# The seam between the two MLP multiplications: four preparations of operands placed behind the last evictions, slice 7's sums behind them, and VectorE's instructions there in the order of the source

## The chip, the cores and the metric

The kernel runs on one core of one Trainium2 chip. The metric is the device time of one execution in microseconds. Engines are named as in the profile: PE is TensorE's matrix multiplication, PEld its weight load, DVE is VectorE, ACT is ScalarE, POOL is GpSimd, SP is SyncE, which here issues the DMA transfers.

## The reference

One layer of a streaming encoder: a normalised input goes through two kinds of attention, an output projection and an MLP with a squared ReLU, each with a residual sum. The sequence has 1024 positions, the model 1024 channels, the MLP 4096 hidden ones, all in float32. The change lies in the MLP alone:

```python
def reference(x, ..., norm2_g, w_ff1, w_ff2, final_norm_g):
    ...
    h = h + jnp.einsum('bsm,md->bsd', y, w_out[layer])
    n2 = rms_norm(h, norm2_g[layer])
    u = jnp.square(jax.nn.relu(jnp.einsum('bsd,df->bsf', n2, w_ff1[layer])))
    h = h + jnp.einsum('bsf,fd->bsd', u, w_ff2[layer])
    return rms_norm(h, final_norm_g)
```

## The kernel before

**Numbers.** Each float32 operand of the MLP is split into two fp16 parts. A high half is a rounded copy that ACT makes; a low half is what remains, made by DVE or POOL. One multiplication then takes three fp16 matmuls (`mm3`). `split` (L1404) issues both: ACT first scales or copies (L1408, L1410), then POOL subtracts (L1412), or DVE subtracts and scales in one instruction (L1414).

**Strassen.** Both MLP multiplications work on 2 x 2 blocks with seven products in place of eight, numbered 1 to 7, in the order 1, 5, 6, 3, 7, 2, 4. The operands of a product are blocks or differences of blocks. `second_operands` (L1387) makes the differences (L1384, DVE), which are called T for the first multiplication's weights and Z for the second's.

**First multiplication.** The hidden channels are cut into eight slices n = 0 to 7. `product1(n, p)` (L1435) runs the 24 matmuls of product p of slice n, from X and W, into a PSUM tile f, and then evicts it. The PSUM tile of product 1 is used again by 6, 7 and 4, that of product 5 by 3; product 2 has its own. Products 1, 5 and 6 are copied by ACT into kept tiles k. Products 3, 7 and 2 are evicted by DVE, which adds a kept tile and takes the largest value (L1473, into topf), and then squares (L1475). Product 4 goes through ACT into v, twice, and DVE finds its largest value (L1471). Behind product 4 stand the slice's **sums**, four additions or subtractions of kept tiles on DVE (L1484 to L1490), and short instructions for the scale (L1495, L1496, L1189). Each finished block of u, the squared activations, is stored to DRAM (ud). The stores stand in SP's queue in the written order, since `queue[0]` is there an `InOrder` object (L151): a wrapper that ties each instruction it issues behind the one before. ACT has the same wrapper during the first multiplication (`act1[0]`, from the ninth product on). DVE hasn't: what is given to it straight is ordered by the scheduler.

**Second multiplication.** `order2` (L1582) lists group g, product p and slice n; four groups of two slices each. One product of one slice takes 24 matmuls from V and U into a chain f_a, f_b or f_c; two slices make the 48 that a row of the trace shows together. DVE adds each finished chain into an accumulator C (`add_up`, L1733). `prepare2(at)` (L1637) makes the **pieces** for entry `at` of `order2`: U from a block u that was loaded from ud, and V from a block of the second weights or a difference Z of two. Both are split as above. U's low half is POOL's work, but DVE's for product 5. `fetch2` loads blocks u, through SP, a few entries ahead.

**The seam.** While slice 7 of the first multiplication runs, the first pieces of the second are made. `FIRST_PIECES` (L47) says behind which product of slice 7 each of the first four is made: entries 0 to 3 are product 1 of slices 0 and 1 and product 5 of slices 0 and 1. `FIRST_LOADS` says the same of the loads and isn't touched. The main loop (L1652 to L1682) calls `prepare1`, which makes the weights W of a product some places ahead, then `product1`, then the rest. After it stand `load_acc` (L1687), which loads the accumulators C, and the groups of the second multiplication.

In names such as k7_6, W7_2, U0_5 or Z1_6 the first number is the slice and the second the product; C001 is half 1 of block (0, 0).

Of the kernel before, what the change touches and what calls it, by code (L numbers as in the profile page):

```python
# [24 lines left out]
NQ = DFF // (4 * P)  # L25
# [20 lines left out]
}  # L46
FIRST_PIECES = {(7, 1): 0, (7, 5): 1, (7, 6): 2, (7, 3): 3}  # L47
START_FILL = 3
A_FILL = 7
B_FILL = [13, 13, 9.5, 9.5] * 2 + [11.25] * 8  # L50
# [15 lines left out]
def kernel(  # L66
# [29 lines left out]
    nc = tc.nc  # L96
# [411 lines left out]
    dve, pool = nc.vector, nc.gpsimd  # L508
# [576 lines left out]
    for j in range(4):  # L1085
        Q, K, V = [], [], []
        fill.add(f"B{j}", in_proj(KB0 + j * P, "k", f"kB{j}", K, None))
        q, v = (QB0 + j * P, "q", f"qB{j}", Q, None), (VB0 + j * P, "v", f"vB{j}", V, None)
# [50 lines left out]
    def flat(t):  # L1139
        return t.rearrange("p a b -> p (a b)")  # L1140

    def page2(shape, name, dt=F32):
        return mp.tile(shape, dt, tag="pg2", bufs=10, name=name)

    def tst(shape, name):
        return main.tile(shape, F32, tag="tst", bufs=TST, name=name)
# [3 lines left out]
    def page16(shape, name, alloc=None):  # L1150
        return (alloc or page)(shape, name, F16)
# [63 lines left out]
    def pair_psum(name):  # L1215
        return mps.tile([P, 2, HALF], F32, tag="ab", bufs=3, name=name)
# [154 lines left out]
    def scaled1(n, *blocks):  # L1371
        up1, left = to_scale1[n]
        for b in blocks:
            if b in left:
                left.remove(b)
                w = w1s[(n, *b)]
                act1[0].activation(w, w, AF.Copy, scale=up1)
# [9 lines left out]
    def second_operands(src, made, p, name, engine, alloc):  # L1387

        if p == 1:
            return src(0, 0)  # L1390
        if p == 2:
            return src(1, 0)
        if p == 3:
            return src(1, 1)
        a, b = {
            5: lambda: (src(0, 1), src(0, 0)),
            6: lambda: (src(1, 1), made[5]),
            7: lambda: (src(1, 1), src(0, 1)),
            4: lambda: (src(1, 0), made[6]),
        }[p]()  # L1400
        made[p] = sum_of(a, b, ALU.subtract, name, engine, alloc)
        return made[p]

    def split(full, name, engine, alloc, up=None):  # L1404
        w = alloc(name)
        w = [w[:, hl] for hl in range(2)]
        if up is not None and engine is pool:
            act1[0].activation(full, full, AF.Copy, scale=up)  # L1408
            up = None
        act1[0].activation(w[0], full, AF.Copy, scale=1.0 if up is None else up)  # L1410
        if up is None:
            engine.tensor_tensor(w[1], full, w[0], ALU.subtract)  # L1412
        else:
            engine.scalar_tensor_tensor(w[1], full, up, w[0], ALU.mult, ALU.subtract)  # L1414
        return w
# [3 lines left out]
    def prepare1(n, p, at):  # L1419
        if n >= NQ or (n, p) in wops:  # L1420
            return
        made = wsum.setdefault(n, {})
        if n:
            scaled1(n, *{1: ((0, 0), (0, 1)), 5: ((0, 1), (1, 1)), 6: ((1, 1), (1, 0))}.get(p, ((1, 0), (0, 1), (1, 1))))
        second = page2 if at < 2 or at > 4 else page1
        t = second_operands(
            lambda i, j: w1s[n, i, j], made, p, f"T{n}_{p}", dve, lambda name: second([P, 4, 2 * P], name)
        )
        wops[n, p] = split(
            t, f"W{n}_{p}", dve if at < 7 and at != 2 else pool, lambda name: page16([P, 2, 4, 2 * P], name), None if n else to_scale1[0][0]  # L1430
        )
# [3 lines left out]
    def product1(n, p):  # L1435
        a, c = chains.setdefault(n, [None, None])
        if p in (1, 5, 2):
            ps = pair_psum(f"f1_{n}_{p}")
            if p == 1:
                chains[n][0] = ps  # L1440
            if p == 5:
                chains[n][1] = ps
        else:
            ps = c if p == 3 else a
        hi, lo = wops.pop((n, p))
        for u in range(2):
            cols = slice(u * P, (u + 1) * P)
            for k in range(4):
                x2 = [X[p][k // 2][:, hl, k % 2] for hl in range(2)]
                mm3(ps[:, u], (hi[:, k, cols], lo[:, k, cols]), x2, k == 0 and p in (1, 5, 2), k == 3, True)  # L1450
                if k % 2:
                    turn()
        while stores:
            stores.pop(0)()
        kept = saved.setdefault(n, {})
        ps = flat(ps)
        if p in (1, 5, 6):
            if p == 5 and n:
                kept[p] = tst([P, 2 * HALF], f"k{n}_{p}")
            else:  # L1460
                kept[p] = page2([P, 2 * HALF], f"k{n}_{p}")
            act1[0].activation(kept[p], ps, AF.Copy)
            return
        v = tst([P, 2 * HALF], f"v{n}") if p == 4 else kept[{3: 6, 7: 5, 2: 1}[p]]
        if n not in topf:
            topf[n] = small.tile([P, 4], F32, tag="topf", bufs=2, name=f"topf_{n}")
        top = topf[n][:, {3: 0, 7: 1, 2: 2, 4: 3}[p] :][:, :1]
        if p == 4:
            act1[0].activation(v, ps, AF.Relu)
            act1[0].activation(v, v, AF.Square)  # L1470
            dve.tensor_reduce(top, ps, mybir.AxisListType.X, ALU.max)  # L1471
        else:
            dve.tensor_tensor_reduce(v, ps, v, 1.0, 0.0, ALU.add, ALU.max, top)  # L1473
            if n:
                dve.scalar_tensor_tensor(v, v, 0.0, v, ALU.max, ALU.mult)  # L1475
            else:
                act1[0].activation(v, v, AF.Relu)
                act1[0].activation(v, v, AF.Square)
        if p != 4:
            put(n, {3: 2, 7: 4, 2: 1}[p], v)  # L1480
            return

        u00, u01, u11, u10 = kept[1], kept[6], kept[5], v
        dve.tensor_tensor(u11, u10, u11, ALU.add)  # L1484
        put(n, 5, u11)
        dve.tensor_tensor(u10, u00, u10, ALU.subtract)
        put(n, 7, u10)
        dve.tensor_tensor(u00, u11, u00, ALU.subtract)
        put(n, 6, u00)
        dve.tensor_tensor(u01, u01, u00, ALU.subtract)  # L1490
        put(n, 3, u01)
        if n % GQ == 0:
            topu[n // GQ] = Top(f"u{n // GQ}", NQ + n // GQ, GQ)
        top, col = topf.pop(n), topu[n // GQ].column()
        nc.vector.tensor_reduce(col, top, mybir.AxisListType.X, ALU.max)  # L1495
        nc.vector.tensor_tensor(col, col, down1[n], ALU.mult)  # L1496
        if n % GQ == GQ - 1:
            topu[n // GQ].gather()
# [138 lines left out]
    def prepare2(at):  # L1637
        if at >= len(order2) or order2[at][1:] in ready2:
            return
        g, p, n = order2[at]  # L1640
        ready2.add((p, n))
        alloc = page if at <= 3 * GQ else page3
        high = lambda name: page16([P, 2, 2, HALF], name, alloc)
        temp = lambda name: alloc([P, 2, HALF], name, F32)
        a = u2s.pop((n, p))
        b = second_operands(lambda i, j: w2s[n, i, j], made_b.setdefault(n, {}), p, f"Z{n}_{p}", dve, temp)
        ops2[n, p] = (
            split(a, f"U{n}_{p}", dve if p == 5 else pool, high, uup[n]), split(b, f"V{n}_{p}", dve, high, up2[g])
        )

    queue[0] = InOrder(nc.sync)
    for at, (n, p) in enumerate(order1):  # L1652
        if at == 8:
            act1[0] = InOrder(nc.scalar)
        if p == (1 if n > 1 else 5) and n:
            load1(n + 1)
        ahead1 = at + (AHEAD1 + 1 if at < AT_ONCE else AHEAD1)

        behind = (n, p) == (0, 2)
        if ahead1 < len(order1) and not behind:  # L1660
            prepare1(*order1[ahead1], ahead1)
        product1(n, p)
        for work in chores.get((n, p), ()):
            combined(*work)
            if behind and work[0] == 5:
                prepare1(*order1[ahead1], ahead1)
        if 0 < n < NQ - 1:
            if p == 3:
                see1(n + 1)
            if p == 7:  # L1670
                scale1(n + 1)
        if p == 3 and n and n % GQ == 0:
            scale_of_u(n // GQ - 1)
        if at > 6:
            look2(at, p != 1)
        for i, blocks in FIRST_LOADS.get((n, p), ()):
            if i is not None:
                fetch2(i)
            for tile2 in blocks:
                load2w(*tile2)  # L1680
        if (n, p) in FIRST_PIECES:
            prepare2(FIRST_PIECES[n, p])  # L1682
    assert not to_see and not on_way and not to_scale
    act1[0] = nc.scalar
    acc = {}

    def load_acc(i, j):  # L1687
# [147 lines left out]
    g, p, n0 = order2[-GQ]  # L1835
# [104 lines left out]
```

## Time and profile before

| What | Value |
|---|---|
| Time, median of 3 runs | 1032.37 us (1030.7 to 1033.74) |
| The profiled execution's own time | 1034.48 us |
| Its span, first to last instruction | 1032.7 us |
| Mean granted TensorE clock | 0.994 |
| DMA, mean over the span | 194 GB/s |

The profile shows one execution. In a row of the timeline stand the start, the length in us, the engine, the line, the operation, the tiles it writes and reads ("out<-in", numbers left out), and the count of instructions that were drawn together. Brackets at the end give the idle time of the engine before the row and what ended it: "[1.74 <-POOL W L1412]" means that the engine stood still for 1.74 us until POOL had written W in line 1412. Rows of one engine overlap a little, since its instructions are pipelined: the next begins shortly before the length given has passed. The columns of the windows are told where they are shown.

### The profile page before, as it was taken

What the parts mean: (1) busy time and instruction counts of PE and PEld (TensorE: products, weight loads), DVE (VectorE), ACT (ScalarE), POOL (GpSimd) and SP (SyncE); (2) the same over time, 40 slices, a digit from 0 to 9 for tenths busy, and PEclk for the clock granted to TensorE, in tenths of its full rate; (3) what the DMA queues carried; (4) which work ended last, traced back from release to release, by engine and by line L of the source; (5) the groups of instructions that cost most, each with busy time, mean ns of one, the idle gap of its engine ahead of it and who ended that gap; (6) DMA issues with size and microseconds to landing.
All of it is one profiled execution on the core that took longest, in us unless ns stands there. A gap on an engine that the chain in (4) does not pass through costs nothing. (4 is left out here: it accounts for less than half of the span.)

```text
span 1032.7 us, 14046 instructions
## 1 busy us (share of the span) xinstructions
PE 997.6 (97%) x4818; PEld 590.7 (57%) x4818; DVE 805.6 (78%) x1288; ACT 650.5 (63%) x1060; POOL 448.9 (43%) x341
## 2 busy tenths in 40 slices
PE   9999999999979999989999999999899999999997
PEld 7888887777756668644444444444344444444443
DVE  5576787867675738995989999979886887686976
ACT  8676766766576745676646655756286655557446
POOL 0466665242452472106335444446163243345333
PEclk9999999999989999999999999999999999999999
DMA  9944527999999894205778668738699454443004
GB/s 355 267 126 130 139 77 186 192 211 228 211 248 225 201 304 159 86 21 183 252 257 285 218 228 288 248 141 304 223 299 401 142 181 137 169 162 123 1 1 163
DMA packets 150567, 200.63 MB, mean 194 GB/s; under 512 B 78688, under 2 KB 96224, under 8 KB 150496
## 3 DMA queue, kind: packets, MB, share of 16 engines
q1 hardware_dynamic: 150352, 199.47, 64.0%
q8 instruction: 38, 0.62, 0.3%
q14 instruction: 33, 0.27, 0.1%
q10 hardware_dynamic: 144, 0.26, 0.1%
HBM read 120.01 MB, written 42.99 MB: 158 GB/s over the span
## 5 line engine op out<-in xcount | busy, mean ns | idle before, releaser
L179 PE MATMUL f<-X,W 128*128 128x512 f16 x1344 | 294.5, 381 | 6.2 <-DVE topf L1473 3.9
L179 PEld LDWEIGHTS <-W 128*128 128x128 f16 x1344 | 131.6, 98 | 164.0 <-issue 7.5
L179 PEld LDWEIGHTS <-U 128*128 128x128 f16 x1356 | 132.4, 98 | 160.6 <-ACT V L1410 1.8
L1412 POOL TENSOR_TENSOR U<-u,U 128x1024 f16<-128x1024 f32 x48 | 120.9, 2531 | 167.7 <-ACT U L1410 157.3
L179 PE MATMUL f_a<-V,U 128*128 128x512 f16 x756 | 165.3, 379 | 0.9 <-DVE C L1733 0.9
L1412 POOL TENSOR_TENSOR W<-T,W 128x1024 f16<-128x1024 f32 x29 | 73.4, 2532 | 82.6 <-ACT W L159 49.4
L1412 POOL TENSOR_TENSOR W<-w,W 128x1024 f16<-128x1024 f32 x21 | 49.4, 2353 | 90.1 <-ACT W L159 69.2
L1408 ACT ACTIVATE u<-u,uupn 128x1024 f32<-128x1024 f32 x46 | 52.1, 1144 | 56.2 <-DMA u<-ud 55.3
L179 PE MATMUL f_c<-V,U 128*128 128x512 f16 x384 | 84.2, 379 | 1.4 <-DVE C L1733 1.4
L1414 DVE SCALAR_TENSOR_TENSOR V<-Z,up,V 128x1024 f16<-128x1024 f32 x32 | 52.3, 1638 | 28.2 <-ACT V L1410 23.3
L631 ACT ACTIVATE P_B<-P_B,nm_B 128x640 f32<-128x640 f32 (+2 forms) x64 | 44.2, 691 | 32.0 <-DVE nm_B L628 16.5
L1410 ACT ACTIVATE U<-u 128x1024 f16<-128x1024 f32 x46 | 48.1, 1045 | 25.6 <-DVE Z L1384 11.3
L179 PE MATMUL op_A<-w_o,y 128*128 128x512 f32 x192 | 58.6, 430 | 5.7 <-DVE ts_vB L441 5.1
L876 DVE SCALAR_TENSOR_TENSOR H_B<-P_B,rc_B,H_B 128x640 f16<-128x640 f32 (+2 forms) x64 | 50.8, 822 | 13.7 <-ACT H_B L871 13.3
L179 PE MATMUL ip_qB<-nT,w_qB 128*128 128x512 f32 x192 | 53.8, 406 | 1.1 <-DVE t_kB L415 1.0
L1414 DVE SCALAR_TENSOR_TENSOR V<-w,up,V 128x1024 f16<-128x1024 f32 x24 | 42.9, 1791 | 14.8 <-ACT V L1410 7.8
L179 PE MATMUL ip_kB<-nT,w_kB 128*128 128x512 f32 x192 | 53.7, 405 | 0.0
L179 PE MATMUL ip_vB<-nT,w_vB 128*128 128x512 f32 x192 | 51.3, 400 | 0.0
L159 ACT ACTIVATE w<-w,up 128x1024 f32<-128x1024 f32 x24 | 26.7, 1137 | 38.5 <-DVE up L1162 38.5
L179 PE MATMUL ip_qA<-nT,w_qA 128*128 128x512 f32 x192 | 50.5, 397 | 0.3 <-DVE VA L185 0.3
L1410 ACT ACTIVATE V<-Z,up 128x1024 f16<-128x1024 f32 x30 | 34.1, 1137 | 25.4 <-DVE Z L1384 24.8
L871 ACT ACTIVATE H_B<-P_B,rc_B 128x640 f16<-128x640 f32 (+2 forms) x64 | 40.8, 685 | 9.9 <-DVE rc_B L868 4.5
(295 smaller groups left out, 2007.1 us busy)
## 6 DMA issues: line engine op xcount, KB each, us to landing
w<-in_w_ff_dram SPq DMA_DIRECT2D x64, 512.0 KB, 7.2
u<-ud SPq DMA_DIRECT2D x56, 512.0 KB, 5.7
ud<-k SPq DMA_DIRECT2D x48, 512.0 KB, 3.6
m<-in_w_ff_dram SPq DMA_DIRECT2D x32, 512.0 KB, 5.9
KkB<-t_kB SPq DMA_DIRECT2D x32, 256.0 KB, 5.1
xr<-in_x_dram SPq DMA_DIRECT2D x8, 512.0 KB, 9.2
st_o<-in_w_out_dram SPq DMA_DIRECT2D x8, 512.0 KB, 4.3
h<-in_x_dram SPq DMA_DIRECT2D x8, 512.0 KB, 4.9
```

What stands on the lines that cost most here:

```text
L159: ins = getattr(self.engine, op)(*args, **kw)
L179: pe(nc.tensor.matmul(*args, **kw))
L631: nc.scalar.activation(pr, pr, AF.Exp, bias=nm, scale=-1.0, accum_out=sm)
L871: nc.scalar.activation(hi, q, AF.Copy, scale=rc)
L876: nc.vector.scalar_tensor_tensor(lo, q, rc, hi, ALU.mult, ALU.subtract)
L1408: act1[0].activation(full, full, AF.Copy, scale=up)
L1410: act1[0].activation(w[0], full, AF.Copy, scale=1.0 if up is None else up)
L1412: engine.tensor_tensor(w[1], full, w[0], ALU.subtract)
L1414: engine.scalar_tensor_tensor(w[1], full, up, w[0], ALU.mult, ALU.subtract)
```

## The change

Three things are moved, and nothing is added or taken away. Entries 2 and 3 of the pieces (product 5 of slices 0 and 1) are made behind products 2 and 4 of slice 7, no longer behind 6 and 3. The sums of a slice stand in a function `finish1`, called at once for slices 0 to 6; slice 7's are called behind its last pieces. From ahead of slice 7's product 7 to the end of the loop, `dve` is an `InOrder` object, so what it issues in that stretch keeps the written order.

```diff
-FIRST_PIECES = {(7, 1): 0, (7, 5): 1, (7, 6): 2, (7, 3): 3}
+FIRST_PIECES = {(7, 1): 0, (7, 5): 1, (7, 2): 2, (7, 4): 3}
...
             put(n, {3: 2, 7: 4, 2: 1}[p], v)
             return
 
+        last_sums.append(lambda: finish1(n, kept, v))
+        if n < NQ - 1:
+            last_sums.pop()()
+
+    last_sums = []
+
+    def finish1(n, kept, v):
+
         u00, u01, u11, u10 = kept[1], kept[6], kept[5], v
         dve.tensor_tensor(u11, u10, u11, ALU.add)
...
             prepare1(*order1[ahead1], ahead1)
+        if (n, p) == (NQ - 1, 7):
+            dve = InOrder(nc.vector)
         product1(n, p)
...
         if (n, p) in FIRST_PIECES:
             prepare2(FIRST_PIECES[n, p])
+        if (n, p) == (NQ - 1, 4):
+            last_sums.pop()()
     assert not to_see and not on_way and not to_scale
     act1[0] = nc.scalar
+    dve = nc.vector
```

**VectorE, from product 3's eviction of slice 7 on.** ISA rows are the evictions (the short one reads the largest value), "k<-k" the squares, U and V the low halves of pieces. In the kernel before:

```order
L1414 SCALAR_TENSOR_TENSOR U0_5_7055<-u0_5_6944,uupn_0_5570,U0_5_7055 128x1024
L1473 ISA k7_6_7045,topf_7_7088<-f1_7_5_6962,k7_6_7045 128x1024
L1473 ISA topf_7_7088 128x1
L1414 SCALAR_TENSOR_TENSOR V0_5_7058<-Z0_5_7053,up2_0_5795,V0_5_7058 128x1024
L1475 SCALAR_TENSOR_TENSOR k7_6_7045<-k7_6_7045 128x1024
L1414 SCALAR_TENSOR_TENSOR U1_5_7093<-u1_5_6948,uupn_1_5572,U1_5_7093 128x1024
L1414 SCALAR_TENSOR_TENSOR V1_5_7096<-Z1_5_7091,up2_0_5795,V1_5_7096 128x1024
L1473 ISA k7_5_6987,topf_7_7088<-f1_7_1_6913,k7_5_6987 128x1024
L1473 ISA topf_7_7088 128x1
L1475 SCALAR_TENSOR_TENSOR k7_5_6987<-k7_5_6987 128x1024
L1473 ISA k7_1_6942,topf_7_7088<-f1_7_2_7131,k7_1_6942 128x1024
L1473 ISA topf_7_7088 128x1
```

In the changed kernel, where instructions that the wrapper issues carry line 159 (U0_6 and so on follow further down):

```order
L1473 ISA k7_6_7045,topf_7_7080<-f1_7_5_6962,k7_6_7045 128x1024
L1473 ISA topf_7_7080 128x1
L1475 SCALAR_TENSOR_TENSOR k7_6_7045<-k7_6_7045 128x1024
L159 ISA k7_5_6987,topf_7_7080<-f1_7_1_6913,k7_5_6987 128x1024
L159 ISA topf_7_7080 128x1
L159 SCALAR_TENSOR_TENSOR k7_5_6987<-k7_5_6987 128x1024
L159 ISA k7_1_6942,topf_7_7080<-f1_7_2_7115,k7_1_6942 128x1024
L159 ISA topf_7_7080 128x1
L159 SCALAR_TENSOR_TENSOR k7_1_6942<-k7_1_6942 128x1024
L159 TENSOR_TENSOR Z0_5_7143<-w2_0_01_6946,w2_0_00_6901 128x1024
L159 SCALAR_TENSOR_TENSOR U0_5_7145<-u0_5_6944,uupn_0_5570,U0_5_7145 128x1024
L159 SCALAR_TENSOR_TENSOR V0_5_7148<-Z0_5_7143,up2_0_5795,V0_5_7148 128x1024
```

The evictions of products 3, 7 and 2 (k7_6, k7_5, k7_1) stand together now, with no piece of product 5 between them, and the pieces follow. Then come topf's reduction, Z1_5, U1_5 and V1_5, and after them the four sums. Behind the sums the two instructions on C000 and C001 now stand ahead of Z0_6 and Z1_6; before, Z0_6 stood first.

**ScalarE, at the same place.** U and V are high halves of pieces, W those of the first multiplication's weights, k7_6 the copy of product 6, and u a block that is scaled in place. Before:

```order
L159 ACTIVATE W7_7_7018<-T7_7_7016 128x1024
L159 ACTIVATE k7_6_7045<-f1_7_1_6913 128x1024
L159 ACTIVATE U0_5_7055<-u0_5_6944,uupn_0_5570 128x1024
L159 ACTIVATE V0_5_7058<-Z0_5_7053,up2_0_5795 128x1024
L159 ACTIVATE W7_2_7061<-w1_7_10_6618 128x1024
L159 ACTIVATE U1_5_7093<-u1_5_6948,uupn_1_5572 128x1024
L159 ACTIVATE V1_5_7096<-Z1_5_7091,up2_0_5795 128x1024
L159 ACTIVATE W7_4_7101<-T7_4_7099 128x1024
L1408 ACTIVATE u0_6_7007<-u0_6_7007,uupn_0_5570 128x1024
L1408 ACTIVATE u1_6_7051<-u1_6_7051,uupn_1_5572 128x1024
L159 ACTIVATE v7_7184<-f1_7_1_6913 128x1024
```

In the changed kernel:

```order
L159 ACTIVATE W7_7_7018<-T7_7_7016 128x1024
L159 ACTIVATE k7_6_7045<-f1_7_1_6913 128x1024
L159 ACTIVATE W7_2_7053<-w1_7_10_6618 128x1024
L159 ACTIVATE W7_4_7085<-T7_4_7083 128x1024
L1408 ACTIVATE u0_6_7007<-u0_6_7007,uupn_0_5570 128x1024
L1408 ACTIVATE u1_6_7051<-u1_6_7051,uupn_1_5572 128x1024
L159 ACTIVATE U0_5_7145<-u0_5_6944,uupn_0_5570 128x1024
L159 ACTIVATE V0_5_7148<-Z0_5_7143,up2_0_5795 128x1024
L159 ACTIVATE v7_7176<-f1_7_1_6913 128x1024
L159 ACTIVATE v7_7176<-v7_7176 128x1024
L159 ACTIVATE U1_5_7182<-u1_5_6948,uupn_1_5572 128x1024
L159 ACTIVATE V1_5_7185<-Z1_5_7180,up2_0_5795 128x1024
```

W7_2 and W7_4 come right behind the copy of product 6, and the pieces of product 5 come behind the scaling of u0_6 and u1_6; U1_5 and V1_5 stand behind both instructions on v.

**ScalarE, in the second multiplication's second group.** The changed code doesn't name this place; the scheduler puts the rows there. Before:

```order
L1410 ACTIVATE U3_5_7782<-u3_5_7633,uupn_3_6168 128x1024
L1410 ACTIVATE V3_5_7785<-Z3_5_7780,up2_1_6182 128x1024
L1408 ACTIVATE u2_4_7960<-u2_4_7960,uupn_2_6166 128x1024
L1410 ACTIVATE U2_6_7818<-u2_6_7672 128x1024
L1410 ACTIVATE V2_6_7822<-Z2_6_7816,up2_1_6182 128x1024
L1410 ACTIVATE U3_6_7855<-u3_6_7705 128x1024
L1408 ACTIVATE u3_4_7997<-u3_4_7997,uupn_3_6168 128x1024
L1410 ACTIVATE V3_6_7859<-Z3_6_7853,up2_1_6182 128x1024
L1410 ACTIVATE U2_3_7892<-u2_3_7740 128x1024
L1408 ACTIVATE u4_1_8036<-u4_1_8036,uupn_4_6771 128x1024
```

In the changed kernel:

```order
L1408 ACTIVATE u3_2_7923<-u3_2_7923,uupn_3_6168 128x1024
L1410 ACTIVATE V3_5_7785<-Z3_5_7780,up2_1_6182 128x1024
L1410 ACTIVATE U2_6_7818<-u2_6_7672 128x1024
L1408 ACTIVATE u2_4_7960<-u2_4_7960,uupn_2_6166 128x1024
L1410 ACTIVATE V2_6_7822<-Z2_6_7816,up2_1_6182 128x1024
L1408 ACTIVATE u3_4_7997<-u3_4_7997,uupn_3_6168 128x1024
L1410 ACTIVATE U3_6_7855<-u3_6_7705 128x1024
L1408 ACTIVATE u4_1_8036<-u4_1_8036,uupn_4_6771 128x1024
L1410 ACTIVATE V3_6_7859<-Z3_6_7853,up2_1_6182 128x1024
L1410 ACTIVATE U2_3_7892<-u2_3_7740 128x1024
```

U2_6 has moved from behind u2_4 to ahead of it, and u4_1 from behind V3_6 to ahead. From V2_3 on, which comes next, ACT's order is that of before, and in the third and fourth groups DVE's is too. The orders of POOL and SP are unchanged throughout.

## The prediction

> **What bounds the kernel now.** I began with the page's busy shares:
>
> ```profile
> PE 997.6 (97%) x4818; PEld 590.7 (57%) x4818; DVE 805.6 (78%) x1288; ACT 650.5 (63%) x1060; POOL 448.9 (43%) x341
> ```
>
> PE is busy for 97% of the span, so a change elsewhere counts only where PE waits or runs slowly. The second view is PE's timeline around the seam of the two MLP multiplications, and then its rows to the end.
>
> ```profile
> 700.11 16.14 PE L179 MATMUL f<-X,W 128*128 128x512 f16 x74
> 717.99 4.92 PE L179 MATMUL f<-X,W 128*128 128x512 f16 x22 [1.74 <-POOL W L1412]
> 726.81 6.91 PE L179 MATMUL f<-X,W 128*128 128x512 f16 x24 [3.90 <-DVE topf L1473]
> 733.56 10.52 PE L179 MATMUL f_a<-V,U 128*128 128x512 f16 x48
> ```
>
> ```profile
> 754.28 10.52 PE L179 MATMUL f_a<-V,U 128*128 128x512 f16 x48
> ...
> 920.04 10.52 PE L179 MATMUL f_a<-V,U 128*128 128x512 f16 x48
> ...
> 961.48 10.52 PE L179 MATMUL f_b<-V,U 128*128 128x512 f16 x48
> 973.38 10.52 PE L179 MATMUL f_c<-V,U 128*128 128x512 f16 x48 [1.38 <-DVE C L1733]
> ```
>
> The 74 matmuls end with slice 7's product 7. Product 2 (717.99) waited 1.74 us for POOL's low half of W, product 4 (726.81) 3.90 us for DVE's eviction of product 7, whose PSUM tile it writes into. Then the second multiplication runs without a wait up to 972. Product 4 was slow as well. From 733.56 to 754.28, 20.72 us, 96 matmuls run, so 24 take 5.18; its 24 took 6.75 (726.81 to 733.56). The windows say why; the columns after the length and five busy times are granted clock, DMA share and GB/s:
>
> ```profile
> 726.80:729.00 2.20, 2.19 (x6) 0.80 (x6) 2.20 (x2) 0.00 (x0) 0.00 (x0) 0.50 0.07 28
> 729.00:731.00 2.00, 2.00 (x9) 0.76 (x8) 1.38 (x3) 0.00 (x0) 0.00 (x0) 0.74 0.57 231
> ```
>
> The clock was 0.50 and then 0.74: 2.20 x 0.50 + 2.00 x 0.26 = 1.6 us lost. The seam costs PE 1.74 + 3.90 + 1.57 (6.75 less 5.18) = **7.21 us**.
>
> Why they came late stands in the rows of ACT, POOL and DVE:
>
> ```profile
> 705.49 1.02 ACT L159 ACTIVATE k<-f 128x1024 f32<-128x1024 f32 x1
> 710.84 1.15 ACT L159 ACTIVATE U<-u,uupn 128x1024 f16<-128x1024 f32 x1 [4.32 <-DMA u<-ud]
> 713.33 1.15 ACT L159 ACTIVATE V<-Z,up 128x1024 f16<-128x1024 f32 x1 [1.34 <-DVE Z L1384]
> 714.38 1.04 ACT L159 ACTIVATE W<-w 128x1024 f16<-128x1024 f32 x1
> ```
>
> ```profile
> 706.61 3.10 POOL L1412 TENSOR_TENSOR W<-T,W 128x1024 f16<-128x1024 f32 x1
> 715.50 2.43 POOL L1412 TENSOR_TENSOR W<-w,W 128x1024 f16<-128x1024 f32 x1 [5.79 <-ACT W L159]
> ```
>
> ```profile
> 715.86 3.15 DVE L1414 SCALAR_TENSOR_TENSOR U<-u,uupn,U 128x1024 f16<-128x1024 f32 x1
> 718.93 1.21 DVE L1473 CUSTOM_DVE_ANT_0 k<-f,k 128x1024 f32<-128x1024 f32 x1
> 720.08 2.01 DVE L1414 SCALAR_TENSOR_TENSOR V<-Z,up,V 128x1024 f16<-128x1024 f32 x1
> ...
> 725.54 1.21 DVE L1473 CUSTOM_DVE_ANT_0 k<-f,k 128x1024 f32<-128x1024 f32 x1
> ...
> 727.93 1.22 DVE L1473 CUSTOM_DVE_ANT_0 k<-f,k 128x1024 f32<-128x1024 f32 x1
> 729.19 1.23 DVE L1475 SCALAR_TENSOR_TENSOR k<-k 128x1024 f32<-128x1024 f32 x1
> ```
>
> ACT works in the written order: W of product 2 (714.38) stood behind the pieces U0_5 and V0_5, which waited 4.32 us for a transfer and 1.34 for Z. DVE's eviction of product 7 (725.54) stood behind four low halves of pieces, although its product had ended at 716.25.
>
> **The change part by part.** No instruction is added or removed; only places move, so nothing is paid for work itself.
>
> *ACT and POOL.* W7_2 follows ACT's copy that ends at 706.51 and takes 1.04, so it is there at 707.6. POOL is free at 709.7 (706.61 + 3.10), and the low half is done at 712.1, before product 2 can begin (717.99 - 1.74 = 716.25). W7_4 follows with 2.43 to 3.10 more, 715.2 at the latest, against 721.2, where product 4 begins. The 1.74 goes; late next is nothing in POOL.
>
> *DVE's evictions.* Product 3's can run before 716.25, product 7's from there, 1.21, to 717.5, with 3.7 us in hand before product 4. The 3.90 goes, and with no such wait the slow clock. The only risk is an instruction ahead that waits. Only the low half of V1_1 stands there; it stood ahead of U0_5's (715.86) too, so it was done before product 7 ended. PE's new times: product 2 at 716.25, product 4 at 721.2, second multiplication at 733.56 - 7.21 = **726.35**. Its product 5 follows at 736.7 (second slice 741.9), product 6 at 747.1 (752.3).
>
> *The pieces behind.* They had lain beside the wait; now DVE must do them between the last eviction and 736.7. These rows price them.
>
> ```profile
> 722.64 1.15 ACT L1408 ACTIVATE u<-u,uupn 128x1024 f32<-128x1024 f32 x1 [2.76 <-DMA u<-ud]
> 733.76 1.02 ACT L159 ACTIVATE v<-f 128x1024 f32<-128x1024 f32 x1 [9.97 <-PE f L179]
> ```
>
> ```profile
> 734.82 1.23 DVE L1471 TENSOR_REDUCE topf<-f 128x1 f32<-128x1024 f32 x1 [4.40 <-ACT v L159]
> 737.21 3.03 DVE L1486 TENSOR_TENSOR v<-k,v 128x1024 f32<-128x1024 f32 x1
> 742.67 1.22 DVE L1384 TENSOR_TENSOR Z<-w,Z 128x1024 f32<-128x1024 f32 x1
> 743.81 1.28 DVE L1733 SCALAR_TENSOR_TENSOR C<-f_a,down,C 128x1024 f32<-128x1024 f32 x1
> 746.14 1.28 DVE L1414 SCALAR_TENSOR_TENSOR V<-Z,up,V 128x1024 f16<-128x1024 f32 x1
> ```
>
> ```profile
> 736.89 2.26 POOL L1412 TENSOR_TENSOR U<-u,U 128x1024 f16<-128x1024 f32 x1 [15.89 <-ACT U L1410]
> ```
>
> Eviction and square of product 2 take 2.49 (727.93 to 729.19 + 1.23), from 721.2 to 723.7. Z0_5 comes to 724.8. U0_5 needs ACT's high half, which now stands behind the scaling of u1_6 (722.64, held by its transfer): 723.8 + 1.15 = 724.9, low half 726.2. V0_5 to 727.4, the reduction to 728.6 (ACT's v follows PE's 726.35 by 1.02), Z1_5, U1_5 and V1_5 to 732.2. All are there before 736.7, and the second slice's before 741.9: 9 us of cover.
>
> *The sums behind those.* Reduction and sums took 734.82 to 742.67, 7.85 us, of which the sums alone 6.71 (734.82 + 1.14 = 735.96); one took 3.03 beside POOL's low half (736.89). They end at 732.2 + 6.7 = 738.9, 3.8 us earlier than 742.67, while PE is 7.2 earlier. Two C additions (1.28 each) now come first, then two Z (1.22), ACT's high half (1.15) and V0_6's low half (1.28): 738.9 + 2.6 + 2.4 + 1.3 = 745.2, against 747.1. The lead falls from 754.28 - 747.42 = 6.9 to **1.9 us**, so still no wait.
>
> *What follows the sums: the feed of u.* SP issues the loads of u behind the sums' stores, ACT scales what landed, then DVE or POOL make low halves:
>
> ```profile
> 743.20 1.72 SPq L159 DMA_DIRECT2D u<-ud  x2
> ```
>
> ```profile
> 749.13 1.15 ACT L1408 ACTIVATE u<-u,uupn 128x1024 f32<-128x1024 f32 x1 [3.05 <-DMA u<-ud]
> ...
> 811.28 1.15 ACT L1408 ACTIVATE u<-u,uupn 128x1024 f32<-128x1024 f32 x1 [3.43 <-DMA u<-ud]
> ```
>
> ```profile
> 751.35 1.28 DVE L1414 SCALAR_TENSOR_TENSOR V<-Z,up,V 128x1024 f16<-128x1024 f32 x1 [2.74 <-ACT V L1410]
> ...
> 915.70 1.29 DVE L1414 SCALAR_TENSOR_TENSOR V<-Z,up,V 128x1024 f16<-128x1024 f32 x1 [1.22 <-ACT V L1410]
> ...
> 969.82 2.22 DVE L1414 SCALAR_TENSOR_TENSOR V<-Z,up,V 128x1024 f16<-128x1024 f32 x1 [1.08 <-ACT V L1410]
> 971.96 2.46 DVE L1733 SCALAR_TENSOR_TENSOR C<-f_b,down,C 128x1024 f32<-128x1024 f32 x2
> ```
>
> All of it moves up by 3.8 only. V1_6 is then done at 751.35 + 1.28 - 3.8 = 748.8, against 752.3. The smallest lead I found later is 8.2 (917.0 against the second slice of 920.04, at 925.2); 3.4 less leaves 4.8. Where no lead is left is 972: PE waits 1.38 for C of f_b, which stands behind a V (969.82) at the end of the same feed. If the feed lags 3.4 there, the wait becomes 4.8. Against that stands the new order of ACT in the second group: U2_6 comes ahead of u2_4, whose scaling waited 3.43 for its load (811.28). Work that stood behind this wait can start up to 3.4 earlier, and that is the lag. The edit of ACT's order is thus worth between 0 and 3.4 in the feed; I take 3.4, since the row shows the wait and from there on both versions have one order. The wait at 972 stays near 1.4.
>
> **Sum.** 1034.48 - 7.2 = 1027.3 for the profiled execution (1.8 us beside its span stay). That execution lies 2.1 above the median of the runs; on the median, 1032.37 - 7.2 = **1025.2 us**.
>
> **The rivals.**
>
> *Early pieces late.* For: the lead of 1.9 at product 6. Each DVE operation that meets POOL loses 1.8 (3.03 against 1.22); two more of these, 3.6, or a transfer that lands as much later, make PE wait 1.7, up to 3: 1026.9 to 1028.2. Against: one meeting is in the sum already, and POOL has only U0_6 and U1_6 to make there. [...]
>
> *The feed keeps its lag.* ACT's new order brings nothing: the wait at 972 grows by 3.4 to 4.8, more than the 3.90 after which the clock was 0.50, so 1.6 is lost again. Saving 7.2 - 3.4 - 1.6 = 2.2: 1030.2. For: the feed starts only 3.8 earlier. Against: the 3.43 wait, and leads of 4.8 and more before it. [...]
>
> *Slower: DVE's fixed order stalls on u1_6.* Everything behind Z0_5, the sums and SP's stores too, now waits for U0_5's high half, and that for u1_6's transfer. PE's wait at product 6 is the delay less 1.9. Beyond 8.7 of wait plus 1.6 of clock, 10.3, the version is over 3.1 slower. That takes a landing 10.6 us later than 722.64, past 733: about 1036. The windows, with the columns above:
>
> ```profile
> 718.00:721.00 3.00, 3.00 (x14) 1.36 (x15) 3.00 (x4) 1.60 (x2) 2.47 (x1) 1.00 1.05 395
> 721.00:723.00 2.00, 1.91 (x9) 0.78 (x8) 2.00 (x2) 0.36 (x1) 0.01 (x1) 1.00 0.19 76
> ```
>
> For it, the transfer engines were full (1.05) shortly before the landing, and slice 7's stores now join them earlier. Against it, 0.19 right after: little is queued that could push it 10 us.
>
> *It doesn't do what it says.* An eviction still comes late because the V1_1 ahead of it waits; only the 1.74 goes: 1030.6.
>
> **Chances and range.** Forecast 0.58, early pieces late 0.12, feed lag 0.13, only the 1.74 gone 0.07, slower 0.10. A measurement tells 0.3%, 3.1 us, from no change: faster is below 1029.3, slower above 1035.5. The first two are faster (0.70), the next two the same (0.20), the last slower (0.10). The forecast's own range is 1022 to 1026.9: down by the 1.38 at 972, if DVE comes free there, and the 1.7 by which the runs lie below their median, up by the first rival's beginning. With the two "same" cases the range is 1022.0 to 1030.6; what lies outside is the slower case and the edges.
>
> **What would show it.** Right: products 2 and 4 without a wait, 24 matmuls in 5.2, granted clock 1.00 until 733; eviction of product 7 at 716 to 718; the sums' end 3 to 5 us earlier; V0_6 before product 6; about 1.4 of wait at the last group's f_c. Wrong: a wait at product 6 or above 3 us near 965, or U0_5's high half after 728.

## The result, and the profile after

| | Before | After |
|---|---|---|
| Time, median (lowest to highest, runs) | 1032.19 us (1030.7 to 1033.74, 4) | 1024.28 us (1023.81 to 1024.83, 4) |
| Ratio, 95% interval | | 0.9924 (0.9910 to 0.9938) |
| Span of the profiled execution | 1032.7 us | 1023.0 us |

Two more measurements of the same changed kernel, in later groups of runs, gave ratios of 0.9929 (0.9916 to 0.9942) and 0.9942 (0.9924 to 0.9961). The prediction was 1025.2 us, a ratio of 0.9931.

PE's timeline (start, length, what, and in brackets a wait and what ended it). First the row of the matmul `all_w` in the kernel before, whose next rows the prediction shows, and then the changed kernel:

```profile
700.00 0.27 PE L182 MATMUL all_w<-ident,top_w 128*128 128x128 f32 x1
```

```profile
697.82 0.27 PE L182 MATMUL all_w<-ident,top_w 128*128 128x128 f32 x1
697.93 26.06 PE L179 MATMUL f<-X,W 128*128 128x512 f16 x120
723.83 10.52 PE L179 MATMUL f_a<-V,U 128*128 128x512 f16 x48
734.19 10.52 PE L179 MATMUL f_c<-V,U 128*128 128x512 f16 x48
744.55 10.52 PE L179 MATMUL f_a<-V,U 128*128 128x512 f16 x48
```

```profile
963.72 10.52 PE L179 MATMUL f_c<-V,U 128*128 128x512 f16 x48 [1.45 <-DVE C L1746]
```

The three groups with two waits have become one row of 120 matmuls without any. From `all_w`, which stands ahead of everything that the change moves, to the first f_a it was 733.56 - 700.00 = 33.56 us and is 723.83 - 697.82 = 26.01: **7.55 us less**. From the first f_a to the end of the span it was 299.1 us and is 299.2. The other 2.18 us between the spans lie ahead of `all_w`, in unchanged work. Over the profiles of this study that start varies from 696.9 to 700.3, so this part is an execution's own scatter.

The clock is 1.00 throughout, from 697.9 to 733; here is one window (length, five busy times, clock, DMA share, GB/s):

```profile
717.00:720.00 3.00, 3.00 (x16) 1.35 (x15) 1.31 (x2) 0.63 (x1) 0.00 (x0) 1.00 1.05 409
```

ACT's and POOL's rows of the two weights:

```profile
704.23 1.05 ACT L159 ACTIVATE W<-w 128x1024 f16<-128x1024 f32 x1
708.71 1.06 ACT L159 ACTIVATE W<-T 128x1024 f16<-128x1024 f32 x1 [3.42 <-DVE T L1384]
...
720.42 1.15 ACT L1408 ACTIVATE u<-u,uupn 128x1024 f32<-128x1024 f32 x1 [2.79 <-DMA u<-ud]
721.48 1.13 ACT L159 ACTIVATE U<-u,uupn 128x1024 f16<-128x1024 f32 x1
```

```profile
707.49 3.10 POOL L1412 TENSOR_TENSOR W<-w,W 128x1024 f16<-128x1024 f32 x1
710.56 3.11 POOL L1412 TENSOR_TENSOR W<-T,W 128x1024 f16<-128x1024 f32 x1
```

W7_2 and W7_4 are finished at 710.6 and 713.7; product 2 begins at 713.5 (723.83 less two products of 5.18) and product 4 at 718.7, so they are 2.9 and 5.0 us early. DVE's timeline from there, of which the second and third row shown are the evictions of products 7 and 2:

```profile
711.61 1.21 DVE L1473 CUSTOM_DVE_ANT_0 k<-f,k 128x1024 f32<-128x1024 f32 x1
...
714.68 1.21 DVE L159 CUSTOM_DVE_ANT_0 k<-f,k 128x1024 f32<-128x1024 f32 x1
...
718.85 1.22 DVE L159 CUSTOM_DVE_ANT_0 k<-f,k 128x1024 f32<-128x1024 f32 x1 [1.69 <-PE f L179]
...
722.65 1.28 DVE L159 SCALAR_TENSOR_TENSOR U<-u,uupn,U 128x1024 f16<-128x1024 f32 x1 [0.17 <-ACT U L159]
...
728.69 1.28 DVE L159 SCALAR_TENSOR_TENSOR V<-Z,up,V 128x1024 f16<-128x1024 f32 x1
729.89 3.15 DVE L159 TENSOR_TENSOR k<-v,k 128x1024 f32<-128x1024 f32 x1
...
736.73 2.47 DVE L1746 SCALAR_TENSOR_TENSOR C<-f_a,down,C 128x1024 f32<-128x1024 f32 x2
...
741.61 1.29 DVE L1414 SCALAR_TENSOR_TENSOR V<-Z,up,V 128x1024 f16<-128x1024 f32 x1
```

Evictions are 711.61, 714.68 and 718.85. DVE now waits for PE (1.69) where PE waited for DVE. The U behind them waited 0.17 for ACT, which had waited for the transfer of u1_6.

### The profile page after: what moved, and what is told of

Same layout as the page of the kernel before. It is cut to its first block, busy times and chain, and to the rows that moved or that the text cites. A ratio compares the mean times of both kernels' runs of the same rounds, so it can differ in the third digit from the quotient of the medians.

```text
span 1023.0 us, 14043 instructions
## 1 busy us (share of the span) xinstructions
PE 994.0 (97%) x4818; PEld 589.4 (58%) x4818; DVE 804.0 (79%) x1288; ACT 650.2 (64%) x1060; POOL 448.1 (44%) x341
## 5 line engine op out<-in xcount | busy, mean ns | idle before, releaser
L1412 POOL TENSOR_TENSOR U<-u,U 128x1024 f16<-128x1024 f32 x48 | 118.3, 2476 | 168.0 <-ACT U L1410 151.8
L1414 DVE SCALAR_TENSOR_TENSOR V<-Z,up,V 128x1024 f16<-128x1024 f32 x30 | 47.6, 1586 | 28.8 <-ACT V L1410 20.3
L1414 DVE SCALAR_TENSOR_TENSOR V<-w,up,V 128x1024 f16<-128x1024 f32 x24 | 46.7, 1948 | 11.4 <-ACT V L1410 6.6
L179 PE MATMUL op_B<-w_o,y 128*128 128x512 f32 x192 | 46.8, 396 | 0.2 <-ACT o L1072 0.2
```

Of the source, the lines that this page charges most:

```text
L179: pe(nc.tensor.matmul(*args, **kw))
```

## The experiments

Each row below is one profiled execution, and the time and ratio are against the kernel before in the same rounds. "Seam" goes from `all_w` to the first f_a, "rest" from there to the span's end, "wait" is that at the last group's f_c.

| Run | Seam | Rest | Wait | Time | Ratio (95%) |
|---|---|---|---|---|---|
| before | 33.56 | 299.1 | 1.38 | | |
| the change | 26.01 | 299.2 | 1.45 | 1024.28 | 0.9924 (0.9910 to 0.9938) |
| e1_no_inorder | 29.23 | 299.6 | 1.94 | 1029.00 | 0.9947 (0.9930 to 0.9965) |
| e2_sums_front | 26.01 | 297.6 | 0 | 1024.22 | 0.9899 (0.9879 to 0.9919) |
| e3_act_order_before | 26.01 | 302.7 | 2.80 | 1027.93 | 0.9932 (0.9910 to 0.9954) |
| e4_c_first | 26.01 | 297.5 | 0 | 1024.13 | 0.9898 (0.9880 to 0.9916) |
| e5_change_again | 26.01 | 299.3 | 1.57 | 1025.46 | 0.9929 (0.9916 to 0.9942) |
| e6_weights_front | 33.98 | 299.7 | 1.90 | 1033.47 | 1.0005 (0.9995 to 1.0015) |
| e7_second_back | 29.58 | 299.8 | 2.14 | 1028.30 | 0.9955 (0.9941 to 0.9969) |
| e8_two_swaps | 26.01 | 296.8 | 0 | 1023.79 | 0.9911 (0.9897 to 0.9925) |
| e9_one_swap | 26.01 | 299.0 | 1.31 | 1025.51 | 0.9927 (0.9907 to 0.9947) |
| e10_sums_front_again | 26.01 | 297.6 | 0 | 1023.88 | 0.9917 (0.9904 to 0.9930) |
| e11_change_third | 26.01 | 300.0 | 2.22 | 1026.07 | 0.9942 (0.9924 to 0.9961) |

e1 to e4, e5 to e8 and e9 to e11 ran together. The seam repeats to a hundredth, while times scatter by a few microseconds with what happens ahead of `all_w`. Effects under 3 us are therefore read from the stages, and the ratios only have to agree.

**The seam, part by part.** e6 moves the weights of products 2 and 4 alone, in the kernel before:

```diff
         product1(n, p)
+        if (n, p) == (NQ - 1, 6):
+            for ahead in range(ahead1 + 1, len(order1)):
+                prepare1(*order1[ahead], ahead)
```

> The kernel before with one thing moved: the weights W of slice 7's products 2 and 4 are prepared right behind product 6, ahead of the pieces of product 5, so that ACT and POOL make them in time. DVE still makes all four low halves of the pieces ahead of product 7's eviction. Theory (the two waits do not add: the eviction's time is set by DVE's own row of work, so a product 2 that begins earlier only waits longer behind it): the 1.74 us at product 2 go, the wait at product 4 grows by about as much, to 5 to 6 us, the clock drops behind it; 0 to 0.7 us less than the kernel before, ratio 0.9993 to 1.000. Rival (the waits add, each is worth its length): 1.74 us and the drain of 0.17 go, ratio 0.998.

PE, DVE and the clock in e6:

```profile
725.49 7.81 PE L179 MATMUL f<-X,W 128*128 128x512 f16 x24 [5.34 <-DVE topf L1473]
```

```profile
724.22 1.21 DVE L1473 CUSTOM_DVE_ANT_0 k<-f,k 128x1024 f32<-128x1024 f32 x1
```

```profile
720.10:725.40 5.30, 0.05 (x1) 0.00 (x0) 5.30 (x6) 1.50 (x2) 0.00 (x0) 0.84 0.30 123
725.49:727.50 2.01, 2.01 (x5) 0.69 (x5) 2.01 (x2) 0.00 (x0) 0.00 (x0) 0.50 0.00 0
```

Product 2 no longer waits, product 4 waits 5.34 in place of 3.90, and its 24 matmuls take 7.81 in place of 6.91, since the clock has fallen to 0.50. Nothing is won: the eviction comes when DVE has done its row of work, whenever PE arrives. The theory holds for the wait and the clock. The seam is 33.98, 0.42 longer than before, where 0 to 0.7 less was expected: the eviction came 0.47 earlier, counted from `all_w` (25.07 against 25.54), and the low clock took 0.90 more (7.81 against 6.91).

e7 moves one entry of the two, in the kernel before:

```diff
-FIRST_PIECES = {(7, 1): 0, (7, 5): 1, (7, 6): 2, (7, 3): 3}
+FIRST_PIECES = {(7, 1): 0, (7, 5): 1, (7, 6): 2, (7, 4): 3}
```

> The kernel before with one piece moved: only entry 3 (product 5 of slice 1) is made behind product 4; entry 2 stays behind product 6, slice 7's sums and DVE's scheduling as before. W of product 2 still stands behind U0_5 and V0_5 on ACT, so its wait of 1.7 us stays; two low halves fewer stand ahead of product 7's eviction, so it comes 2.4 us earlier. Theory (each low half of a piece ahead of the eviction costs its 1.2 us, and the clock drops only behind a long wait): product 4 waits about 1.5 us, without a drop of the clock, so 3.6 us are lost against the changed kernel and 3.9 of the 7.5 won, ratio to the kernel before 0.996. Rival (the clock drops behind any wait of some length, or the feed loses what the seam wins): 0.998 or above.

```profile
714.88 4.92 PE L179 MATMUL f<-X,W 128*128 128x512 f16 x22 [1.73 <-POOL W L1412]
721.32 5.34 PE L179 MATMUL f<-X,W 128*128 128x512 f16 x24 [1.51 <-DVE topf L1473]
```

PE's rows show the two waits that were expected, 1.73 and 1.51, and product 4's 24 matmuls in 5.34, as in e1, where the clock is 1.00. The seam is 29.58 - 26.01 = 3.57 longer than in the changed kernel, that is 1.73 + 1.51 and 0.33 more: each of the two adds about 0.17 beside its own length, the end of the last matmul before it, which otherwise lies under the next (in the changed kernel f_a ends at 734.35, 723.83 + 10.52, and f_c starts at 734.19).

e1 takes the wrapper from the changed kernel:

```diff
-        if (n, p) == (NQ - 1, 7):
-            dve = InOrder(nc.vector)
...
-    dve = nc.vector
```

> The change without the wrapper on DVE: pieces of product 5 behind products 2 and 4, slice 7's sums written behind them, but the scheduler orders DVE. It puts the low halves of U0_5 and V0_5 ahead of the eviction of product 7 again, and ACT's high half of U0_5 still stands behind the scaling of u1_6. Theory (the order of the evictions is what is worth most, and only the wrapper gives it): with the profile of the changed kernel, U0_5's high half is ready at 722.6, the two low halves end at 725.1, the eviction at 726.3, against 718.9 where product 4 could begin. PE waits about 7.4 us there, then runs at a lower clock as before the change (about 1.6 us), so about 9 us are lost: 1033 to 1034 us, slower than the kernel before by about 1. The wait for W of product 2 is gone all the same. Rival (moving the pieces is the gain, the wrapper only tidies): 1024 to 1025 us.

PE's and DVE's rows:

```profile
722.49 5.34 PE L179 MATMUL f<-X,W 128*128 128x512 f16 x24 [3.06 <-DVE topf L1473]
```

```profile
718.82 1.28 DVE L1414 SCALAR_TENSOR_TENSOR U<-u,uupn,U 128x1024 f16<-128x1024 f32 x1
720.01 1.28 DVE L1414 SCALAR_TENSOR_TENSOR V<-Z,up,V 128x1024 f16<-128x1024 f32 x1
721.21 1.22 DVE L1473 CUSTOM_DVE_ANT_0 k<-f,k 128x1024 f32<-128x1024 f32 x1
```

The direction was right, the size wrong: two low halves stand ahead of the eviction again, but the wait is 3.06, not 7.4, and the clock is 1.00 behind it, from 722.49 to 727.60. The expectation misread ACT's order, in which U0_5 and V0_5 of this kernel stand ahead of u1_6's scaling and wait for no transfer. The wrapper is worth 29.23 - 26.01 = 3.2 us of the 7.55; without it the kernel is still faster than before.

**The sums' place.** e2 and e10 keep all but the sums' move:

```diff
-        last_sums.append(lambda: finish1(n, kept, v))
-        if n < NQ - 1:
-            last_sums.pop()()
+        finish1(n, kept, v)
...
-        if (n, p) == (NQ - 1, 4):
-            last_sums.pop()()
```

> The change with slice 7's sums at their old place in the source, ahead of U1_5 and V1_5, wrapper kept. The sums end about 3.6 us earlier (733 in place of 736.7 in the changed kernel's profile), V1_5 is ready at about 736.7, against 739.4, where product 5's second slice begins. Theory (the sums' place decides nothing, since the feed of u is paced by what PE frees): within 0.1% of the changed kernel, 1023.5 to 1025, the wait at the last group's f_c still 1.4 to 1.5 us. Rival 1 (the feed's late start is what that wait is made of): the wait falls towards 0, 1022.9 us. Rival 2 (the pieces must stand ahead of the sums): PE waits for V1_5 at product 5's second slice, 1 to 4 us, 1025.5 to 1028.

The wait was gone, so Rival 1 held and not the theory. Since one profile might have met a lucky phase, it was run again beside the changed kernel:

> Once more the change with slice 7's sums at their old place in the source, beside the changed kernel in the same rounds, since the first run of it shows no wait at the last group's f_c (297.6 us from the first f_a to the end of the span, 299.2 in the changed kernel). Theory (written behind the pieces, the sums start the feed of u 3.6 us later, and that is the wait of 1.45): 1.6 us less than the changed kernel in the same rounds, and again no wait there. Rival (the first run met a better phase of its transfers): the wait is back, no difference beyond 0.5 us.

> The changed kernel beside the two others of this group. Every theory expects 0.990 to 0.994 of the kernel before, 299.2 to 299.4 us from the first f_a to the end of the span, and 1.4 to 1.6 us of wait at the last group's f_c.

PE in e10, and then in e11:

```profile
952.11 10.52 PE L179 MATMUL f_b<-V,U 128*128 128x512 f16 x48
962.47 7.72 PE L179 MATMUL f_c<-V,U 128*128 128x512 f16 x35
```

```profile
966.97 10.52 PE L179 MATMUL f_c<-V,U 128*128 128x512 f16 x48 [2.22 <-ACT U L1410]
```

Again no wait with the sums in front, and 297.6 us of rest; the changed kernel, with 2.22 in this execution, is above what was expected of it. In the same rounds the medians are 1023.88 and 1026.07, with intervals of the ratio that overlap a little. So of the change's three parts, the sums' move costs some 1.6 us. The scheduler also orders ACT differently in e2 and e10, at some thirty places between V1_6 (there ahead of u0_3) and V2_3, so the 1.6 is that of both together. Where the feed of u runs later is read below.

**The feed.** e3 holds ACT's order, from U0_6 to V2_3, as it was before the change, and e9 turns back only the pair u2_4 and U2_6 (in e9 the list has these two names):

```diff
+    for first, then in zip(ACT_ORDER, ACT_ORDER[1:]):
+        dep = mybir.DependencyInfo(mybir.DependencyClass.NoSync, mybir.DependencyReason.DATA)
+        tc.add_manual_dep(scaled[then].ins, scaled[first].ins.name, dep, reason="program order")
```

> The changed kernel with ACT's order from U0_6 to V2_3 (first and second group of the second multiplication) held as it was before the change. Theory of the prediction (the new order of ACT, U2_6 ahead of u2_4, makes up the feed's lag of 3.4 us): without it the wait at the last group's f_c grows from 1.45 to about 4.8 us and the clock drops behind it (1.6 us): 1029 to 1029.5 us. Rival (the feed is paced by the buffers that PE frees, and catches up by itself where it waits for its loads): the wait stays 1.4 to 1.5 us, 1023.5 to 1025 us.

> The changed kernel with one pair of ACT's order turned back: u2_4's scaling stands ahead of U2_6 again (the scheduler then moves u3_4 and u4_1 back by a place or two as well); the rest of ACT's new order and all of DVE's, POOL's and SP's stay. Theory of the prediction (this pair is what made up the feed's lag): all that the run with the whole old order lost against the changed kernel comes back, 3.4 us from the first f_a to the end of the span (302.7 against 299.3), with a wait of 2.8 us and a slow clock at the last group's f_c; ratio to the kernel before 0.996. Rival (the earlier places of the first and second group, u0_2, u1_4, V3_1, U2_5, decide): the wait stays at 1.4 to 1.6, 299.3 us, ratio 0.9925.

PE in e3, with the clock behind the wait, and then PE in e9:

```profile
777.50 10.52 PE L183 MATMUL f_b<-V,U 128*128 128x512 f16 x48 [0.30 <-DVE C L1750]
...
966.94 12.21 PE L183 MATMUL f_c<-V,U 128*128 128x512 f16 x48 [2.80 <-DVE C L1750]
```

```profile
966.94:968.00 1.06, 1.06 (x5) 0.48 (x6) 1.06 (x2) 0.00 (x0) 1.06 (x2) 1.00 0.00 0
968.00:969.00 1.00, 1.00 (x4) 0.43 (x3) 1.00 (x1) 0.00 (x0) 1.00 (x1) 0.51 0.00 0
```

```profile
965.16 5.12 PE L180 MATMUL f_c<-V,U 128*128 128x512 f16 x23 [1.31 <-ACT V L1411]
```

With the whole old order the rest grows by 3.5 us: 0.30 with its drain, 1.35 more of wait, and 12.21 - 10.52 = 1.69 by the clock. With one pair turned back nothing is lost, though the scaling of u2_4, again ahead of U2_6, waits for its load as it did before the change (3.43 there):

```profile
802.53 1.15 ACT L1409 ACTIVATE u<-u,uupn 128x1024 f32<-128x1024 f32 x1 [3.37 <-DMA u<-ud]
```

The 3.5 of e3 is read from one execution, the slowest of its four (1029.69 against a median of 1027.93). In the same rounds e2 and e4 ran in 1024.22 and 1024.13, 3.7 to 3.8 less, where the stages differ by 5.1. And e3's ratio, 0.9932, lies among the three of the changed kernel (0.9924 to 0.9942). What the old order costs against the changed kernel is thus shown in the stage alone, not in the time.

How late the feed runs can be read from POOL, whose order is the same in all these kernels. Its low halves of U, the third and, some 75 us on, the seventeenth, in the kernel before, the changed one, e3, e9 and e10:

```profile
753.38 5.46 POOL L1412 TENSOR_TENSOR U<-u,U 128x1024 f16<-128x1024 f32 x2 [3.98 <-ACT U L1410]
...
831.48 4.38 POOL L1412 TENSOR_TENSOR U<-u,U 128x1024 f16<-128x1024 f32 x2 [3.10 <-ACT U L1410]
```

```profile
746.73 5.21 POOL L1412 TENSOR_TENSOR U<-u,U 128x1024 f16<-128x1024 f32 x2 [1.84 <-ACT U L1410]
...
821.62 4.38 POOL L1412 TENSOR_TENSOR U<-u,U 128x1024 f16<-128x1024 f32 x2 [4.64 <-ACT U L1410]
```

```profile
748.23 5.21 POOL L1416 TENSOR_TENSOR U<-u,U 128x1024 f16<-128x1024 f32 x2 [1.85 <-ACT U L1414]
...
825.20 4.38 POOL L1416 TENSOR_TENSOR U<-u,U 128x1024 f16<-128x1024 f32 x2 [3.13 <-ACT U L1414]
```

```profile
748.30 5.22 POOL L1413 TENSOR_TENSOR U<-u,U 128x1024 f16<-128x1024 f32 x2 [1.84 <-ACT U L1411]
...
823.42 4.38 POOL L1413 TENSOR_TENSOR U<-u,U 128x1024 f16<-128x1024 f32 x2 [3.71 <-ACT U L1411]
```

```profile
744.00 2.96 POOL L1412 TENSOR_TENSOR U<-u,U 128x1024 f16<-128x1024 f32 x1 [1.31 <-ACT U L1410]
...
818.76 2.13 POOL L1412 TENSOR_TENSOR U<-u,U 128x1024 f16<-128x1024 f32 x1 [6.78 <-ACT U L1410]
```

Counted from each kernel's first f_a (733.56, 723.83, 725.24, 725.40 and 724.19), the third starts at 19.8, 22.9, 23.0, 22.9 and 19.8: in the changed kernel, e3 and e9 the feed is 3.1 us later against PE than before the change. The seventeenth starts at 97.9, 97.8, 100.0, 98.0 and 94.6. Here the changed kernel and e9 have made up all of the lag, e3 only 1.1. The third execution of the changed kernel, e11, made up less, 98.9 (825.20 less 726.31), and had the longer wait of 2.22. So ACT's new order does make up the lag, by 1.1 to 2.2 us more than the old one, but not through the pair that the prediction named.

With the sums in front (e10, and e2 to 0.1 the same) the feed runs 3.1 to 3.2 ahead of the changed kernel's at both places, and the wait is gone. The kernel before starts its third at 19.8 too but is at 97.9 by the seventeenth, so an early start doesn't bring this alone. The work in between is ordered differently, and which of its places matters isn't shown.

**What else waits.** At the last group's f_c the bracket names DVE's C or a piece of ACT; in e9 and e11, where it is ACT's, the first C ends within 0.1 us of that piece. e4 makes one swap on DVE (V7_6's low half is tied behind the first C of f_b); e8 has the same and ties two output rows behind the first C of product 7:

```diff
+            if name == "V7_6":
+                tc.add_manual_dep(ins.ins, first_c[0], dep, reason="program order")
...
+            if tb in (2, 3):
+                tc.add_manual_dep(ins.ins, first_c[1], dep, reason="program order")
```

> The changed kernel with one swap on DVE in the last group: the first C addition of f_b stands ahead of V7_6's low half, not behind it. Theory (the wait of 1.45 us at the last group's f_c is this order on DVE and nothing of the feed): the first half of f_b is finished about 2.6 us before its end, its addition comes before PE needs the bank, the wait and its pipeline drain of 0.17 go: 1.6 us less than the changed kernel, 1022.7 us. [...]

> The changed kernel once more, beside the others of this group and timed in the same rounds. Every theory expects 0.990 to 0.994 of the kernel before, and in the profile no wait at slice 7's products 2 and 4, 26.0 us from the end of the all_w matmul to the first f_a, 1.4 to 1.5 us of wait at the last group's f_c, 0.95 at the last f_a.

> The changed kernel with the swap on DVE that puts the first C addition of f_b ahead of V7_6's low half, and a second: the first C addition of the last group's product 7 stands ahead of the output rows fo_2 and fo_3. Theory (the last two waits of PE in this half, 1.45 and 0.95 us, are DVE's order and nothing else): both go with their drains of 0.17, 2.7 us less than the changed kernel beside it, ratio to the kernel before lower by 0.0026. Rival (what ends last is the chain of the output rows, not PE): only the first swap's 1.6 us show, lower by 0.0016 or less.

PE in e8 at the last f_a, where 0.95 stood:

```profile
1007.20 5.34 PE L179 MATMUL f_a<-V,U 128*128 128x512 f16 x24 [0.17 <-DVE bsf L159]
```

In e4 the rest falls by 1.7 us to 297.5, in e8 by 2.5 against e5, to 296.8 (2.7 was expected; 0.17 stays). In time e8 is 1.67 below e5, with overlapping intervals, so of the second swap only the stage is shown. e8 and e10 have the lowest medians beside the changed kernel in their own rounds, and both are faster than the kernel before beyond their intervals.

## Why the prediction was right, point by point

- **The seam: 7.21 predicted, 7.55 measured.** All three terms (1.74, 3.90 and the clock's 1.57) went together. The 0.34 more is a term that was left out: the drain of 0.17 at each of two waits, which e7 shows by itself (0.33 beside its two waits).
- **No term alone.** The prediction priced a change that removes only the 1.74 at 1030.6 us, as if the waits added. e6 shows that this step was wrong: alone it is worth nothing (1.0005), since it passes into the wait behind it. Without the wrapper (e1) 3.2 of the 7.55 are lost.
- **The pieces and the sums.** With the 2.18 us that this execution was earlier, the prediction had V1_5 finished at 730.0 and the sums at 736.7; the rows give 729.97 (728.69 + 1.28) and 736.73. V0_6 was expected at 743.0 and came at 742.9, 1.65 ahead of product 6 at 744.55, for a lead of 1.9. No piece came late. One sum met POOL's low half (729.65, 2.30 long) and took 3.15, the next, without it, 1.23 (733.07). That each DVE operation beside POOL loses 1.8 is too wide: in the profile before, within POOL's row from 718.53 to 721.01, the eviction at 718.93 took 1.21, as the one at 725.54 did without POOL.
- **A reading that was off.** The row of 74 matmuls is not three products but three and the first two matmuls of product 2 (3 x 24 + 2), so product 2 begins at 715.65 in the time of the profile before, not at 716.25, and product 4 at 720.8, not 721.2. POOL finished W7_4 at 715.9 in that time, not at 715.2 at the latest, as both of its rows took 3.1 and none 2.43. With 5.0 us in hand neither mattered.
- **The feed.** "The wait at 972 stays near 1.4" was right in the first profile (1.45), with 1.57 and 2.22 in two others. The reason given was right in kind, ACT's new order, and wrong in place: the step that named U2_6 ahead of u2_4, worth 3.4, fails in e9. What the whole order makes up is 2.2 us of lag (100.0 in e3 against 97.8), and 1.1 in e11 (98.9). Which of its other places does it wasn't tried. That the total came out so well is therefore luck in this term: the place on which it was argued does nothing.
- **The rival of the feed's lag.** Without the new order the wait was put at 4.8 with 1.6 for the clock, a loss of 5.0. e3 has 2.80 with 1.69, and 3.5 in all, in one execution: the wait grew and the clock fell behind it, to 0.51, as expected, but the wait was mis-sized.
- **The slower rival** didn't come about: u1_6's scaling began at 720.42, which is 722.6 in the time of the profile before, against 722.64, and DVE waited 0.17 for it.
- **Not foreseen:** the sums' move, together with the order of ACT that the scheduler gives with it, costs something, and the wait of 1.4 at the last group's f_c can be removed in two ways, by an earlier feed (e10) or by DVE's order (e4).

## What to carry to other kernels

Before adding up waits of the bound engine, ask of each what sets the moment at which it ends: if that doesn't depend on when the bound engine arrives, an earlier wait that is removed merely lengthens it, and the later one has to go first. An engine that works in a fixed order should do first what the bound engine waits for, and a source order that is right must be enforced where a scheduler may undo it. And a chain that feeds later stages should not be put behind work with ample lead without need, even where no wait shows at that place, since its lag can arrive much later: with the sums in front, a wait over 200 us on was gone.

## What the runs showed of the hardware

The fall of the clock isn't decided by a wait's length alone: it came with waits of 2.80 us (e3), 3.90 (before) and 5.34 (e6), not with 3.06 (e1, 1.00 from 722.49 to 727.60) or 2.22 (e11, 1.00 from 966.97 to 971.00). In e3 it began only 1.06 us after PE had resumed (1.00 until 968.00, then 0.51), while in e6 the mean was down to 0.84 within the wait already. What decides it beside the length isn't shown. The price was 1.57 us before (6.91 less 5.34), 1.69 in e3 (12.21 less 10.52) and 2.47 in e6 (7.81 less 5.34). Of the two waits near 3 us here, the one of 2.80 thus cost 1.69 us more, the one of 3.06 nothing.
